# A hybrid gMLP and sparse-attention layer on one core: where cache pages are gathered and output weights are split

## The chip, the core and the metric

The kernel runs on one core of a Trainium2 chip. The metric is the device time of one launch in microseconds (us), the median of three runs. The core has five engines with a queue each: PE (TensorE, matrix products; PEld is its weight load), DVE (VectorE), ACT (ScalarE), POOL (GpSimd) and SP (SyncE), which here issues the DMA transfers. Each engine works through its own queue in order; semaphores tie the queues together. The program's order on each queue is fixed when the program is built.

## The reference, cut to what matters

One inference step of a single layer: 1024 prompt tokens and 8 sample tokens (one new token each, over 256 cached tokens in 2 pages of 128).

```python
hn = rms_norm(x, norm_g)
u, v, z_a, q, kc, vc, ks, vs, kw, vw, gates, z_b = split(hn @ w_in)   # one projection
# group A (gMLP): layer norm of v, spatial gate in chunks of 128 tokens
vn = layer_norm(v, ln_v_g, ln_v_b)
a_out = u * (tril(w_s) @ vn + b_s) * silu(z_a)
# group B (sparse attention): rotated q, ks, kw; compressed k and v; top blocks; window
kcc, vcc = rope(compress(kc, w_ck, pe_ck)), compress(vc, w_cv, pe_cv)
o_b = g0 * attn(q, kcc, vcc) + g1 * attn(q, selected blocks) + g2 * attn(q, window)
mix = concat(a_out, o_b * silu(z_b))
y = rms_norm(x + mix @ w_out, final_g)
# the sample tokens do the same with their cached pages in front:
#   pages(c) = c[page_table]   -> 8 tokens x 2 pages = 16 pages of the four paged caches
```

Outputs are y for prompt and sample, the new k and v rows of each branch, and the normalised v rows of the sample.

## The kernel before, in words

Every fp32 product is done as a split: a tensor is cast to a high part on ACT, the rest is taken by a subtraction (low part), and PE does three matmuls, high by high, low by high and high by low. The work runs in stages:

- up to about 42 us: x is loaded, transposed and split; the first three feature tiles (u and z of group A) are projected. Feature tiles are 128 output columns over all 1032 tokens, in chunks of 344 tokens (`pf`).
- 42 to 117.7 us, the **q stage**: four feature tiles of q. Their weights come in by `load_w` (L133), two loads of 256 KB a tile (`wst<-in_wF`), into a ring of three raw buffers and nine split ones. Each tile is rotated by `rotate` (L297), for which Cq and Sq (cosines and sines, L288) are loaded, and stored to a scratch in DRAM (`qd`, L314). The v weights (`wst<-in_wTv`, eight loads) are fetched in the same stage.
- 117.7 to 216 us, the **v stage**: nine token tiles `ptv` (eight of 128 tokens, one of samples), each of which gets its layer norm (L425 to L431; POOL multiplies by `lng` and adds `lnb`), is split into vh and vl, and goes through `gate` (L393): matmuls `pg` by the lower triangle of w_s, the bias on DVE (L407), the product with u on POOL, and a store of three quarters of it to a scratch `sd` (L412). The constants lng, lnb and w_s are loaded at L349 to L388, behind the stores of the rotated q.
- 190 to 230 us, the **A stage**: token tiles `pta` with ks and kw, rotated in place; each tile's rows go out at L498 and, for the last four, L500. 230 to 270 us, the **B stage**: token tiles `ptb` with the values, gates and raw compressed branch; its weights are `wst<-in_wTb`, eight loads of 204 KB.
- 270 to 324.6 us, **compress** for k and for v (L620), with feature tiles as filler between its steps (`step`, L614); the cached pages (tile `cA`, from the scratch `cg`) are split by POOL at L642. To 366 us the sample's attention.
- 366 to 480 us, attention of query blocks 0 to 3, with feature tiles as filler. 480 to 510 us, the **exchange**: the features are done, their pools close, and the output weights are loaded and split by `load_wo` (L811) into `woh` and `wol`, which take the place of xh and xl. To the end, query blocks 4 to 7 with output projection units (`pout`) as filler.

The cached pages are picked by a page table. SP reads its 16 entries into registers (L294) and issues, for each page, two gathers of 128 KB from DRAM to DRAM, `cg<-in_cA` (L324) and `kg<-in_cB` (L325), four pairs in each q tile, with the instruction `tc.issue_after(W["dma"].ins)`, that is, behind the last weight load issued. A scheduler places other instructions by its own costs, so the queues' order is seen in the built program only.

Of the kernel before, what the change touches and what calls it, by code (L numbers as in the profile page):

```python
# [12 lines left out]
P = 128  # L13
D = 1024
# [25 lines left out]
def trunk(tc, io, outs):  # L40
# [7 lines left out]
    with ExitStack() as top:  # L48
# [26 lines left out]
        cg = dram.tile([2, P, 16, P], F32, name="cg")  # L75
        kg = dram.tile([2, P, 16, P], F32, name="kg")
        qsd = dram.tile([NB, 24], F32, name="qsd")

# [239 lines left out]
        for t in range(4):  # L318
            qF = f_tiles(t)
            wts = f_weights(8 + t) if t else q_first  # L320

            with tc.issue_after(W["dma"].ins):
                for j in range(4 * t, 4 * t + 4):
                    sy.dma_start(cg[:, :, j, :], io["cA"][bass.ds(prow[j], 1)].rearrange("o k p c -> (o k) p c"))  # L324
                    sy.dma_start(kg[:, :, j, :], io["cB"][bass.ds(prow[j], 1)].rearrange("o p (k c) -> (o k) p c", k=2))  # L325
            for k in range(KT):
                f_k(wts, qF, k)
            if t == 1:
                pt = ps_o("pbs")
                for gp in range(4):  # L330
                    pe.transpose(pt[:, gp * P:(gp + 1) * P], bsx.rearrange("p a b -> p (a b)")[:, gp * P:(gp + 1) * P],
                                 ident)
                v.tensor_copy(bsb, pt.rearrange("p (a b) -> p a b", a=4))
            raw = qp.tile([P, TT], F32, tag="raw", bufs=2, name="raw")
            for a, b in zip(views(raw), qF):
                last = s.copy(a, b)  # L336
            if t:
                rotate(t - 1, raws[-1], last)
            raws.append(raw)
        rotate(3, raws[-1], None)  # L340
        qp_ctx.close()
        wq_ctx.close()


# [48 lines left out]
        def gate(i, vh, vl):  # L393
# [17 lines left out]
            g.tensor_tensor(uz[:, 0, cols], uz[:, 0, cols], sp[:, 0, :], op=ALU.mult)  # L411
            sy.dma_start(sd[1:4, :, cols].rearrange("g p c -> p g c"), sp[:, 1:4, :])  # L412

        vn_s = vp.tile([NB, 512], F32, name="vn_s")
        for i in range(9):
# [16 lines left out]
            if i < 8:  # L432
# [3 lines left out]
                v.tensor_tensor(vl, vt, f32(vh), op=ALU.subtract)  # L436
                gate(i, vh, vl)
            else:
                sy.dma_start(outs[14][0, :, 0, :], vn_s)
# [44 lines left out]
        for i in range(9):  # L484
# [12 lines left out]
            rows = slice(i * P, (i + 1) * P)  # L497
            sy.dma_start(o_ks[rows], ka[:, 0:P])  # L498
            if i >= 4:
# [55 lines left out]
        def feature_tiles(bank):  # L555
# [5 lines left out]
            for n, (what, i, _) in enumerate(todo):  # L561
# [5 lines left out]
                for j in range(3):  # L567
# [13 lines left out]
                    if what == "z":  # L581
                        gt = ftp.tile([P, CH], F32, tag="gt", name="gt")
                        sy.dma_start(gt[:, 0:n_p], sd[i, :, cols])
                    z = ftp.tile([P, CH], F32, tag="z", bufs=2, name="z")
                    th = ftp.tile([P, CH], F32, tag="th", name="th")
# [34 lines left out]
        def compress(kv):  # L620
# [17 lines left out]

            def split(dst, src, e=v):
                hi = dst(Xh)  # L640
                s.copy(hi, src)
                e.tensor_tensor(dst(Xl), src, f32(hi), op=ALU.subtract)  # L642
            split(lambda x: x[:, :, 384:388], pce.rearrange("p a j -> p j a"))
# [9 lines left out]
            for h in range(2):  # L653
                split(lambda x: x[:, :, h * SLOT + 64:h * SLOT + 192].rearrange("p j (a m) -> p a j m", m=8),
                      cA[:, :, h * 64:h * 64 + 64].rearrange("p a (m j) -> p a j m", j=8), g)
            pc = ps_p("pc")
            n = 0
            with step(8 if kv == 0 else 12):
              for half in range(2):
# [135 lines left out]
        sm_ctx.close()  # L795
        left = N_FT - (8 + 12 + 4 + 4 + 4 + 12 + 6 + 4)

# [11 lines left out]
        sy.dma_start(cmpm, io["cmpm"])  # L809

        def load_wo(k):  # L811
            st = wop.tile([P, D], F32, tag="wost", name="wost")
            sy.dma_start(st, io["w_out"][k])
            s.copy(woh[:, k, :], st)
            (g if k % 2 else v).tensor_tensor(wol[:, k, :], st, f32(woh[:, k, :]), op=ALU.subtract)

# [296 lines left out]
        for i, (qb, h, tp) in enumerate(todo):  # L1113
            units = [n_values(q) + 2 for q, _, _ in todo[i:] if (q < EARLY) == (qb < EARLY)]
            if 0 <= i - 4 * EARLY < 3:
                units[0] = 0
            if i == 4 * EARLY + 3:
                held_back = blocks[qb]["last"].ins
# [21 lines left out]
            if qb == EARLY - 1:  # L1140
                for _ in fill:
                    pass
                ft_ctx.close()
                wo_ctx = ExitStack()
                wop = wo_ctx.enter_context(tc.tile_pool(name="wop", bufs=7, side="right", reuse_waits="tile"))
                fg = xp.tile([P, D], F32, tag="row", name="fg")
                sy.dma_start(fg, io["final_g"].partition_broadcast(P))
                woh = xp.tile([P, KT, D], F32R, tag="wh", name="woh")
                wol = xp.tile([P, KT, D], F32R, tag="wl", name="wol")
                for k in range(KT):  # L1150
                    load_wo(k)
                wo_ctx.close()
                mixp = top.enter_context(tc.tile_pool(name="mixp", bufs=2, side="right", reuse_waits="tile"))
# [127 lines left out]
```

## Time and profile before

| | |
|---|---|
| median of three runs | 757.92 us (756.63 to 757.99) |
| the profiled execution: its time, its span | 757.39 us, 755.6 us |
| mean granted clock of PE | 0.959 |
| busy: PE, DVE, ACT, POOL | 689.3, 517.2, 373.9, 297.1 us |
| DMA traffic | 78.70 MB, 104 GB/s over the span |

PE is busy for 91% of the span, so the time is PE's work, plus the stretches in which PE stands still, plus what PE loses where its clock is granted at the lower of its two levels. A view by stretches of time shows which stages have such gaps; the views of waits and of the chain say what ended them. A PEclk of 1.00 in such a row is the full clock of 2.4 GHz, 0.50 would be 1.2 GHz all through.

### The profile page before, as it was taken

The numbers are of one execution on the slowest core, as the hardware profiler recorded it, in microseconds if no ns is written. First come the engines' busy times: TensorE is split into PE (matmuls) and PEld (weight loads), VectorE is DVE, ScalarE is ACT, GpSimd is POOL, SyncE is SP. The second block draws the span as 40 slices with busy tenths as digits, with TensorE's granted clock in tenths as the row PEclk, the third lists the DMA queues.
The fourth block names the chain that finished last, engine by engine and source line by source line (L and its number), as shares of the span: only waits on it lengthen the run. The fifth ranks groups of instructions, "written<-read, shape, count | busy, mean of one in ns | idle before, by whom it ended". The sixth has DMA issues, their size and how long they took to land.

```text
span 755.6 us, 12512 instructions
## 1 busy us (share of the span) xinstructions
PE 689.3 (91%) x4186; PEld 635.3 (84%) x4186; DVE 517.2 (68%) x1470; ACT 373.9 (49%) x882; POOL 297.1 (39%) x274
## 2 busy tenths in 40 slices
PE   9996399879999999799899999868999999999994
PEld 7996398768899999698899999757999898988993
DVE  6622296469966155843399989999878786788753
ACT  8410132114225254212377877787666674676631
POOL 0010143154331017442222444478656554375421
PEclk9998689979999999899999999989999999999997
DMA  9153546502234044262533112445123122212011
GB/s 338 52 183 101 157 135 175 146 19 74 69 116 130 26 166 154 61 234 103 147 112 90 62 48 62 160 171 167 44 65 103 43 59 77 52 67 75 19 55 53
DMA packets 61256, 78.70 MB, mean 104 GB/s; under 512 B 5200, under 2 KB 44736, under 8 KB 60392
## 3 DMA queue, kind: packets, MB, share of 16 engines
q1 hardware_dynamic: 60744, 75.48, 31.8%
q0 software_dynamic: 160, 2.15, 0.7%
q8 instruction: 33, 0.54, 0.3%
q14 instruction: 31, 0.25, 0.1%
q10 hardware_dynamic: 288, 0.27, 0.1%
HBM read 59.46 MB, written 24.71 MB: 111 GB/s over the span
## 4 chain that ended last, share of the span: by engine, by line
PE 62%; DVE 13%; SPq 8%; DMA 6%; issue 5%; ACT 3%; POOL 2%; POOLq 0%; DVEq 0%; ACTq 0%
PE pf L45 13%; PE pout L45 11%; PE o L45 8%; PE pt L928 8%; PE S L45 7%; PE ptb L45 5%; SPq L324 4%; PE ptv L45 2%; PE pta L45 2%; DVE tl L932 1%; SPq L139 1%; DVE Pl L847 1%; SPq L325 1%; PE pc L45 1%; PE pg L45 1%
## 5 line engine op out<-in xcount | busy, mean ns | idle before, releaser
L45 PE MATMUL pf<-xh,whi 128*128 128x344 f32 x384 | 111.9, 333 | 11.9 <-ACT raw L336 5.6
L932 DVE TENSOR_TENSOR tl<-pt,th 128x512 fp32r<-128x512 f32 (+1 forms) x160 | 101.2, 643 | 16.6 <-ACT th L931 16.0
L45 PE MATMUL pf<-xl,whi 128*128 128x344 f32 x384 | 111.9, 328 | 0.0
L45 PE MATMUL pf<-xh,wlo 128*128 128x344 f32 x384 | 111.4, 327 | 0.0
L931 ACT CAST th<-pt 128x512 fp32r<-128x512 f32 (+1 forms) x160 | 84.9, 551 | 42.4 <-PE pt L928 37.4
L905 POOL TENSOR_TENSOR Pw<-Pw,r 128x640 f32<-128x640 f32 (+3 forms) x112 | 78.4, 718 | 39.6 <-DVE r L899 23.5
L45 PE MATMUL pout<-woh,mix 128*128 128x512 f32 (+1 forms) x272 | 88.0, 388 | 2.7 <-ACT mix L965 1.8
L45 PEld LDWEIGHTS pf<-xh,whi 128*128 128x128 f32 x384 | 71.4, 194 | 14.3 <-ACT raw L336 5.9
L905 POOL TENSOR_TENSOR Pl<-Pl,r 128x384 f32<-128x384 f32 (+5 forms) x36 | 49.0, 1361 | 80.2 <-DVE r L899 26.2
L45 PE MATMUL o<-th,v 128*128 128x256 f32 x264 | 75.0, 305 | 2.7 <-DVE oT L941 2.7
L142 ACT CAST whi<-wst 128x512 fp32r<-128x512 f32 (+2 forms) x50 | 28.7, 588 | 90.9 <-DMA wst<-in_wF 28.3
L45 PEld LDWEIGHTS pf<-xl,whi 128*128 128x128 f32 x384 | 72.1, 195 | 0.7 <-DVE xl L205 0.3
L45 PE MATMUL o<-tl,v 128*128 128x256 f32 x264 | 70.1, 291 | 2.5 <-DVE tl L932 2.5
L45 PEld LDWEIGHTS pf<-xh,wlo 128*128 128x128 f32 x384 | 71.4, 193 | 0.7 <-issue 0.4
L851 ACT ACTIVATE Pl<-Pl,nmx 128x128 f32<-128x128 f32 (+7 forms) x64 | 49.8, 778 | 23.3 <-DVE nmx L847 18.0
L45 PEld LDWEIGHTS pout<-woh,mix 128*128 128x128 f32 x272 | 50.9, 191 | 11.7 <-ACT mix L965 2.0
L891 ACT ACTIVATE Pw<-Pw,nmx 128x640 f32<-128x640 f32 (+4 forms) x64 | 44.6, 697 | 27.1 <-DVE nmx L883 26.1
L45 PEld LDWEIGHTS o<-tl,v 128*128 128x128 f32 x264 | 51.0, 193 | 5.9 <-DVE tl L932 4.6
L45 PE MATMUL S<-ksS,q 128*128 128x384 f32 (+5 forms) x192 | 53.0, 362 | 3.2 <-DVE nmx L847 1.8
L45 PE MATMUL S<-kwS,q 128*128 128x384 f32 (+2 forms) x224 | 54.0, 337 | 1.6 <-DVE nmx L847 1.5
L45 PEld LDWEIGHTS o<-th,v 128*128 128x128 f32 x264 | 50.9, 193 | 5.0 <-DVE oT L941 3.4
L143 DVE TENSOR_TENSOR wlo<-wst,whi 128x512 fp32r<-128x512 f32 (+2 forms) x32 | 27.7, 886 | 38.7 <-ACT whi L142 38.6
(338 smaller groups left out, 1713.2 us busy)
## 6 DMA issues: line engine op xcount, KB each, us to landing
q<-qd SPq DMA_DIRECT2D x32, 256.0 KB
wst<-in_wF SPq DMA_DIRECT2D x26, 256.0 KB
raw<-in_xw SPq DMA_DIRECT2D x7, 708.0 KB
wost<-in_w_out SPq DMA_DIRECT2D x8, 512.0 KB
xt<-in_x_prompt SPq DMA_DIRECT2D x8, 512.0 KB
out<-xt SPq DMA_DIRECT2D x7, 512.0 KB
cg<-in_cA SPq DMA_DIRECT2D x16, 128.0 KB
kg<-in_cB SPq DMA_DIRECT2D x16, 128.0 KB
```

Of the source, the lines that this page charges most:

```text
L45: return pe.matmul(out, lhsT, rhs, start=start, stop=stop, skip_group_check=True)
L139: W["dma"] = sy.dma_start(st[:, :n], src)
L142: s.copy(hi[:, :n], st[:, :n])
L143: e.tensor_tensor(lo[:, :n], st[:, :n], f32(hi[:, :n]), op=ALU.subtract)
L324: sy.dma_start(cg[:, :, j, :], io["cA"][bass.ds(prow[j], 1)].rearrange("o k p c -> (o k) p c"))
L325: sy.dma_start(kg[:, :, j, :], io["cB"][bass.ds(prow[j], 1)].rearrange("o p (k c) -> (o k) p c", k=2))
L851: s.activation(Pl[:, 0:L], Pl[:, 0:L], AF.Exp, bias=nmx[:, 0:1], scale=-1.0, accum_out=sums[:, 1:2])
L891: s.activation(Pw[:, 0:nw], Pw[:, 0:nw], AF.Exp, bias=nmx[:, 1:2], scale=-1.0, accum_out=sums[:, 2:3])
L905: g.tensor_tensor(t_[:, a:b], t_[:, a:b], r[:, j:j + 1].to_broadcast((P, b - a)), op=ALU.mult)
L928: pe.transpose(pt[:, ci * 256 + e * P:ci * 256 + (e + 1) * P], src[e][:, col:col + P], ident)
L931: s.copy(th[:, :n], pt[:, :n])
L932: v.tensor_tensor(tl[:, :n], pt[:, :n], f32(th[:, :n]), op=ALU.subtract)
```

## The change

1. The 16 pairs of gathers leave the q stage. A new function `gather(j, behind)` issues pair j behind the store of a v tile's gate (pairs 0 to 7) and behind the o_ks store of an A tile (pairs 8 to 15).
2. The output weights are split in the v stage: `split_wo(half, k)`, twice per v tile, loads 256 KB, casts on ACT, subtracts on POOL and stores both parts to a new DRAM scratch `wod` (16 loads and 32 stores of 256 KB). At the exchange `load_wo` is gone, with its pool `wop`; four loads of 2 MB bring both parts back, ahead of the load of final_g.
3. The page splits of compress go from POOL to DVE; the filler of the second compress (v) is 18 feature units in place of 12.
4. The gate's input buffer `gt` has two buffers in place of one, `z` three in place of two. Two attention units in place of three go without filler behind the exchange.

```diff
+        wod = dram.tile([2, 2, P, KT, 512], F32, name="wod")
...
-            with tc.issue_after(W["dma"].ins):
-                for j in range(4 * t, 4 * t + 4):
-                    sy.dma_start(cg[:, :, j, :], io["cA"][bass.ds(prow[j], 1)].rearrange("o k p c -> (o k) p c"))
-                    sy.dma_start(kg[:, :, j, :], io["cB"][bass.ds(prow[j], 1)].rearrange("o p (k c) -> (o k) p c", k=2))
...
+        def gather(j, behind):
+
+            with tc.issue_after(behind.ins):
+                sy.dma_start(cg[:, :, j, :], io["cA"][bass.ds(prow[j], 1)].rearrange("o k p c -> (o k) p c"))
+                sy.dma_start(kg[:, :, j, :], io["cB"][bass.ds(prow[j], 1)].rearrange("o p (k c) -> (o k) p c", k=2))
...
-            sy.dma_start(sd[1:4, :, cols].rearrange("g p c -> p g c"), sp[:, 1:4, :])
+            st = sy.dma_start(sd[1:4, :, cols].rearrange("g p c -> p g c"), sp[:, 1:4, :])
+            gather(i, st)
+
+        def split_wo(half, k):
+
+            cs_ = slice(half * 512, half * 512 + 512)
+            st = vp.tile([P, 512], F32, tag="wost", bufs=2, name="wost")
+            hi = vp.tile([P, 512], F32R, tag="wohi", bufs=2, name="wohi")
+            lo = vp.tile([P, 512], F32R, tag="wolo", bufs=2, name="wolo")
+            sy.dma_start(st, io["w_out"][k, :, cs_])
+            s.copy(hi, st)
+            g.tensor_tensor(lo, st, f32(hi), op=ALU.subtract)
+            sy.dma_start(wod[half, 0, :, k, :], f32(hi))
+            sy.dma_start(wod[half, 1, :, k, :], f32(lo))
...
                 gate(i, vh, vl)
+                for half in range(2):
+                    split_wo(half, i)
...
-            sy.dma_start(o_ks[rows], ka[:, 0:P])
+            st = sy.dma_start(o_ks[rows], ka[:, 0:P])
+            gather(8 + i, st)
...
-                      cA[:, :, h * 64:h * 64 + 64].rearrange("p a (m j) -> p a j m", j=8), g)
+                      cA[:, :, h * 64:h * 64 + 64].rearrange("p a (m j) -> p a j m", j=8))
...
-            with step(8 if kv == 0 else 12):
+            with step(8 if kv == 0 else 18):
...
-        def load_wo(k):
-            st = wop.tile([P, D], F32, tag="wost", name="wost")
-            sy.dma_start(st, io["w_out"][k])
-            s.copy(woh[:, k, :], st)
-            (g if k % 2 else v).tensor_tensor(wol[:, k, :], st, f32(woh[:, k, :]), op=ALU.subtract)
...
-                sy.dma_start(fg, io["final_g"].partition_broadcast(P))
                 woh = xp.tile([P, KT, D], F32R, tag="wh", name="woh")
                 wol = xp.tile([P, KT, D], F32R, tag="wl", name="wol")
-                for k in range(KT):
-                    load_wo(k)
-                wo_ctx.close()
+                for half in range(2):
+                    for hl, w in enumerate((woh, wol)):
+                        sy.dma_start(f32(w[:, :, half * 512:half * 512 + 512]), wod[half, hl])
+                sy.dma_start(fg, io["final_g"].partition_broadcast(P))
```

SP's queue in the q stage. Before, from the last pair of the first q tile on (`wst` is a raw weight buffer, `cg` and `kg` the scratch for pages, an ISA row prepares a register):

```order
L324 DMA cg<-in_cA 256x128
L325 ISA
L325 DMA kg<-in_cB 256x1x128
L139 DMA wst<-in_wF 128x512 x2
L324 ISA
L324 DMA cg<-in_cA 256x128
L325 ISA
L325 DMA kg<-in_cB 256x1x128
```

The same place of SP's queue after the change, from the last read of the page table to the first stores of rotated q:

```order
L140 DMA wst<-in_wF 128x512 x6
L140 DMA wst<-in_wTv 128x512 x5
L280 DMA ud<-uz 128x1032
L140 DMA wst<-in_wTv 128x512 x3
L289 DMA Cq<-in_Cq 128x1032
L290 DMA Sq<-in_Sq 128x1032
L140 DMA wst<-in_wTa 128x384
L315 DMA qd<-qh 64x8x128 x2
```

No gather is left there; the loads of Cq and Sq stand behind six q weight loads and all eight v weight loads, where before the 16 pairs of gathers, six q weight loads and three v weight loads stood ahead of them.

SP's queue at the end of the A stage. Before, from the store of group A's result on (`ka` holds the rotated rows of a tile):

```order
L440 DMA ad<-uz 128x1024
L412 DMA sd<-sp 128x3x128
L139 DMA wst<-in_wF 128x512 x2
L498 DMA out<-ka 128x128
L500 DMA out<-ka 128x128
L139 DMA wst<-in_wF 128x512 x2
L498 DMA out<-ka 128x128
L500 DMA out<-ka 128x128
L498 DMA out<-ka 128x128
L500 DMA out<-ka 128x128
L139 DMA wst<-in_wTb 128x408
```

After the change, a later piece of the same stretch, around three of the B weight loads:

```order
L515 DMA out<-ka 128x128
L343 ISA
L343 DMA cg<-in_cA 256x128
L344 ISA
L344 DMA kg<-in_cB 256x1x128
L518 DMA out<-ka 128x128
L140 DMA wst<-in_wTb 128x408 x3
L140 DMA wst<-in_wF 128x512
L515 DMA out<-ka 128x128
L343 ISA
L343 DMA cg<-in_cA 256x128
```

Between the last gate's `sd` store and the eighth load of `wst<-in_wTb` stand nine pairs of gathers; before, none.

POOL's queue at the start of the v stage, before the change (`wsl` is the low part of the spatial weights, `vt` a v tile):

```order
L430 TENSOR_TENSOR vt<-vt,lng 128x512 x2
L392 TENSOR_TENSOR wsl<-ws,wsh 128x1024
L431 TENSOR_TENSOR vt<-vt,lnb 128x512 x2
```

And after it (`wolo` is the low part of the output weights):

```order
L445 TENSOR_TENSOR vt<-vt,lng 128x512
L425 TENSOR_TENSOR wolo<-wost,wohi 128x512
L445 TENSOR_TENSOR vt<-vt,lng 128x512
L425 TENSOR_TENSOR wolo<-wost,wohi 128x512
L394 TENSOR_TENSOR wsl<-ws,wsh 128x1024
L446 TENSOR_TENSOR vt<-vt,lnb 128x512 x2
```

Two subtractions of output weights stand ahead of `wsl` and of the additions that end the first tile's norm.

## Rows read from the trace of the kernel before

**Rows 1.** Stretches: us, busy PE, PEld, DVE, ACT, POOL, PEclk, DMA, GB/s.

```profile
68.10:75.00 6.90, 6.65 (x27) 6.37 (x27) 0.00 (x0) 0.00 (x0) 0.00 (x0) 0.66 0.25 77
...
84.30:90.50 6.20, 6.14 (x23) 5.90 (x23) 0.00 (x0) 0.00 (x0) 0.00 (x0) 0.55 0.30 104
...
149.00:156.70 7.70, 0.13 (x2) 0.01 (x1) 0.03 (x1) 1.66 (x2) 7.70 (x6) 0.65 0.00 0
...
156.70:216.00 59.30, 56.93 (x311) 51.19 (x312) 55.84 (x154) 16.03 (x32) 24.83 (x23) 0.96 0.20 56
...
240.00:270.00 30.00, 30.00 (x163) 29.71 (x162) 5.91 (x19) 8.85 (x27) 0.00 (x0) 1.00 0.12 33
...
316.00:324.60 8.60, 8.60 (x34) 8.60 (x35) 2.15 (x3) 0.49 (x1) 3.67 (x4) 0.65 0.25 66
...
480.00:535.00 55.00, 43.75 (x265) 36.93 (x264) 53.87 (x157) 42.68 (x100) 39.51 (x34) 0.91 0.52 170
```

**Rows 2.** Waits of PE, 40 to 325 us: total, times, longest.

```profile
PE pbs L331 <- DVE bsx L295: 9.6, 1, 9.6
...
PE pg L45 <- ACT vh L435: 7.9, 2, 7.6
...
PE pf L45 <- ACT raw L336: 5.6, 1, 5.6
...
PE pc L45 <- DVE Xl L642: 5.5, 1, 5.5
...
PE pf L45 <- DVE uz L277: 5.2, 1, 5.2
```

**Rows 3.** Timeline of SP's queue: start, us, instruction.

```profile
50.52 2.31 SPq L324 DMA_DIRECT2D cg<-in_cA  x1
...
53.88 2.31 SPq L324 DMA_DIRECT2D cg<-in_cA  x1
...
56.38 0.67 SPq L325 DMA_DIRECT2D kg<-in_cB  x1
...
91.68 0.38 SPq L288 DMA_DIRECT2D Cq<-in_Cq  x1
...
139.01 1.02 SPq L349 DMA_DIRECT2D lng<-in_ln_v_g  x1
...
216.09 0.82 SPq L412 DMA_DIRECT2D sd<-sp  x1
...
233.04 0.51 SPq L139 DMA_DIRECT2D wst<-in_wTb  x1
```

**Rows 4.** DMA view from 44 to 56 us, 40 slices.

```profile
DMA  9000590154530241021118611111111187111111
...
GB/s 666 0 0 0 219 1533 0 55 185 150 120 75 3 77 121 58 15 63 43 44 56 265 181 55 43 44 43 43 43 44 43 44 242 222 48 44 43 44 43 43
```

**Rows 5.** Timeline of DVE around the rotation of q.

```profile
108.88 1.22 DVE L301 TENSOR_TENSOR raw<-raw,Cq 128x1032 f32<-128x1032 f32 x1
...
129.56 3.45 DVE L301 TENSOR_TENSOR raw<-raw,Cq 128x1032 f32<-128x1032 f32 x1
```

**Rows 6.** POOL's norm products by line: min/median/max ns, first to last.

```profile
L430 POOL TENSOR_TENSOR vt<-vt,lng x8: 1258/1292/1470, 150.0 to 201.9; 128x512 f32<-128x512 f32 x8
```

**Rows 7.** Timeline of DVE in the compress stage.

```profile
302.12 5.63 DVE L675 TENSOR_TENSOR low<-low,Sc 64x384 f32<-64x384 f32 x1
```

**Rows 8.** The tile woh: its splits at the exchange.

```profile
L814 ACT CAST woh<-wost x8: 1047/1066/1077, 489.3 to 502.6; 128x1024 fp32r<-128x1024 f32 x8
...
L815 DVE TENSOR_TENSOR wol<-wost,woh x4: 1607/2178/3416, 491.5 to 504.8; 128x1024 fp32r<-128x1024 f32 x4
...
L815 POOL TENSOR_TENSOR wol<-wost,woh x4: 2355/2378/2387, 493.2 to 508.2; 128x1024 fp32r<-128x1024 f32 x4
```

**Rows 9.** The chain of waits, 205 to 275 us.

```profile
239.99 29.97 PE ptb L45 x161
```

**Rows 10.** DMA view from 490 to 495 us.

```profile
DMA packets 574, 2.09 MB, mean 418 GB/s; under 512 B 64, under 2 KB 64, under 8 KB 574
```

More of the change, by code (lines that the diff above doesn't have):

```diff
@@ L581, in feature_tiles @@
                     if what == "z":
-                        gt = ftp.tile([P, CH], F32, tag="gt", name="gt")
+                        gt = ftp.tile([P, CH], F32, tag="gt", bufs=2, name="gt")
                         sy.dma_start(gt[:, 0:n_p], sd[i, :, cols])
-                    z = ftp.tile([P, CH], F32, tag="z", bufs=2, name="z")
+                    z = ftp.tile([P, CH], F32, tag="z", bufs=3, name="z")
                     th = ftp.tile([P, CH], F32, tag="th", name="th")
@@ L637, in compress, with split @@
             Xl = cx2.tile([P, 8, NSLOT], F32R, tag="Xl", name="Xl")
-            def split(dst, src, e=v):
+            def split(dst, src):
                 hi = dst(Xh)
                 s.copy(hi, src)
-                e.tensor_tensor(dst(Xl), src, f32(hi), op=ALU.subtract)
+                v.tensor_tensor(dst(Xl), src, f32(hi), op=ALU.subtract)
             split(lambda x: x[:, :, 384:388], pce.rearrange("p a j -> p j a"))
@@ L795, in trunk @@
         sm_ctx.close()
-        left = N_FT - (8 + 12 + 4 + 4 + 4 + 12 + 6 + 4)
+        left = N_FT - (8 + 18 + 4 + 4 + 4 + 12 + 6 + 4)
         mk = top.enter_context(tc.tile_pool(name="mk", bufs=1, reuse_waits="tile"))
@@ L1114, in trunk @@
             units = [n_values(q) + 2 for q, _, _ in todo[i:] if (q < EARLY) == (qb < EARLY)]
-            if 0 <= i - 4 * EARLY < 3:
+            if 0 <= i - 4 * EARLY < 2:
                 units[0] = 0
-            if i == 4 * EARLY + 3:
+            if i == 4 * EARLY + 2:
                 held_back = blocks[qb]["last"].ins
@@ L1143, in trunk @@
                 ft_ctx.close()
-                wo_ctx = ExitStack()
-                wop = wo_ctx.enter_context(tc.tile_pool(name="wop", bufs=7, side="right", reuse_waits="tile"))
                 fg = xp.tile([P, D], F32, tag="row", name="fg")
-                sy.dma_start(fg, io["final_g"].partition_broadcast(P))
                 woh = xp.tile([P, KT, D], F32R, tag="wh", name="woh")
                 wol = xp.tile([P, KT, D], F32R, tag="wl", name="wol")
-                for k in range(KT):
-                    load_wo(k)
-                wo_ctx.close()
+                for half in range(2):
+                    for hl, w in enumerate((woh, wol)):
+                        sy.dma_start(f32(w[:, :, half * 512:half * 512 + 512]), wod[half, hl])
+                sy.dma_start(fg, io["final_g"].partition_broadcast(P))
                 mixp = top.enter_context(tc.tile_pool(name="mixp", bufs=2, side="right", reuse_waits="tile"))
```

## The prediction

> **What bounds the kernel now.** I read the table of stretches first [rows 1], since the share of a busy engine over the whole span hides where it stands still. PE is busy through most rows; the gaps lie in four places: the q stage (two rows from 68.1 to 90.5 us, at a granted clock of 0.66 and 0.55), the start of the v stage (149 to 156.7 us, PE busy for 0.13 of 7.7 us), the end of compress (clock 0.65) and the exchange with the first blocks behind it (43.75 of 55 us). The waits of PE say what ended the gaps [rows 2]: in the q stage three single waits of 5.2, 9.6 and 5.6 us, all behind a weight that came late; at the first gate 7.6 us for vh; in compress 5.5 us for Xl. SP's timeline shows why the weights were late [rows 3]: a cg gather holds SP for 2.31 us, its kg for 0.67, and the next pair starts 3.36 us after the last (the cg rows at 50.52 and 53.88). Sixteen pairs cost 16 × 3.36 = 54 us of SP's queue, all ahead of the weights of the next q tile and of Cq.
>
> **Part 1, the q stage.** The queue after the change holds weights alone. The three waits, 20.4 us, have then no cause. PE also loses to its clock: 6.65 us at 0.66 and 6.14 us at 0.55 would be done in 4.4 and 3.4 us at full clock, which is 5.0 us [rows 1]. That is 25.4 us on PE up to the first v tile. The chain of waits runs another way, through SP: Cq, issued at 91.68, feeds the rotation, behind whose last stores lng is issued at 139.01, and the first gate matmul follows at 156.7, the end of the 149 row [rows 1, 3]. After the change Cq stands behind six q and eight v weight loads; the last of these needs a raw buffer, and through it the split weights of the second q tile. PE had that tile nearly done at 62.6 us, before the first of its waits, so I put Cq at about 65 us, 26.7 us earlier. Both ways give 25 to 27; I take −27. Bounds: −16, if Cq waits until the third tile frees its buffers (a tile is 72 matmuls, some 12 us by the 4.4 us for the first row's 27), and −30, if the 7.6 us at the first gate shrinks as well. Against it: on POOL two subtractions now stand ahead of wsl in the order. The nearest rows are POOL's products of the same shape, 1292 ns [rows 6]: 2 × 1.29 = +2.6 us, since POOL was busy through all of 149 to 156.7 [rows 1] and PE waits for it there.
>
> **Part 2, the v stage.** It gets 48 DMAs of 256 KB (2 × 8 loads, 4 × 8 stores), 16 casts on ACT, 16 subtractions on POOL, and eight gather pairs. ACT is 16 of 59 us busy there, so the casts are free. The DMAs: at the 418 GB/s of the best stretch [rows 10] 0.26 MB takes 0.63 us, and 48 take 30 us in a stage of 59 with a DMA share of 0.20. They fit, unless the gathers stand in their way: eight pairs hold SP for 27 us. The POOL subtractions can hurt, for DVE is busy for 55.84 of 59.3 us [rows 1] and is the engine that PE follows there. A DVE product of 128x1032 takes 1.22 us alone and 3.45 beside POOL [rows 5], and a DVE product in compress took 5.63 us while POOL was in a split [rows 7]. So each of 16 subtractions may hold DVE up by anything from nothing to its own 1.29 us: 0 to 20.6 us. POOL already has 24.8 us of work there and DVE still gets 94% busy, so part of the existing lock is in that number, and of the new one DVE's single-input instructions and PSUM reads hide much. I take +5, from 0 to +12, and keep +20 as the far end.
>
> The Trainium skill speaks to this place: "SBUF — State Buffer", section "Who interferes with whom", says that a DVE instruction with two SBUF inputs contends with a GpSimd instruction that reads SBUF, and that whoever issues first holds the shared port for its whole instruction. The trace agrees [rows 5, 7]. By that rule in full the term would be the far end, 20.6 us, and the sum 759.6 (rival E).
>
> **Part 3, the A stage.** Here the change adds a wait. Behind the last `sd` store (216.09 before; call it T) SP had little to do, and it issued the last weight load of the B stage at 233.04, T + 17 [rows 3]; at 239.99 the weight was split and PE ran on for 29.97 us without a gap [rows 9], to T + 54. In the order after the change nine pairs stand between the two: 9 × 3.36 = 30.2 us. Beside them SP has some 14 row stores, four B and four feature weight loads at about 0.4 to 0.5 us each, 11 us, and waits that were inside the 17: T + 41 to T + 47, I take 44. With the same 7 us for landing and splitting, PE gets the last weight at T + 51. It does not stand still all that time: in the order three of nine `pta` tiles and 77 of the 208 `ptb` matmuls stand ahead of the first that needs this weight. The other 131 take 131 × 29.97 / 161 = 24.4 us: T + 75.4, against T + 54. That is +22 us (rounded up from 21.5). PE's own work up to there is about 22 us, so some 25 us of waiting lie bare and the clock may fall in them. Bounds: +10, if row stores waited on PE before and the gathers now fill these waits; +28, if the clock falls and late pages hold up compress.
>
> The gathers are slow for a reason that the move doesn't touch. During a pair the DMA share is 0.1 and the rate 43 to 44 GB/s [rows 4]; 131 KB at 43.5 GB/s is 3.0 us, which is the pace of the pairs. The skill's "DMA: Bandwidth & Descriptors", section "Why a DMA increments its semaphore by 16 and not by 1", says that a transfer is spread over the largest number of engines, up to 16, that divides the slowest dimension of both of its sides; a gather's is 2, so two engines, and the trace agrees with 0.1 of 16. This speaks against the change: by it a pair costs SP the same 3.4 us wherever it stands.
>
> **Part 4, compress.** Without POOL's splits the DVE product of 5.63 us falls back to under 1.2 us (a larger one alone took 1.22 [rows 5]), and PE's wait of 5.5 us for Xl goes [rows 2, 7]; after it PE worked 8.60 us at a clock of 0.65, 3.0 us lost [rows 1]. Together −8.5 at most; the four page splits on DVE, at the 1.22 us of a product of that size [rows 5], give 4.9 back, of which I leave 1.5 on the path: −7, from −8.5 to 0. The six extra feature units move work forward and are nothing by themselves; they fill what gap is left.
>
> **Part 5, the exchange.** PE is idle for 11.3 us of the 55 and loses about 5 to the clock (0.91) [rows 1]. DVE is busy for 53.87 of 55: it is the bound. The splits there cost DVE 4 × 2.18 = 8.7, POOL 4 × 2.38 = 9.5 and ACT 8 × 1.07 = 8.5 us [rows 8], and all go: −9 by DVE's share. In place of 4.2 MB SP fetches 8.4 MB; at 418 GB/s [rows 10] 20 us in place of 10, hidden because the first output projection comes only when attention has taken up the place behind. Bounds: −16 (the whole gap), and +5 if the q load queued behind the 8.4 MB is late by half of the extra 10 us.
>
> **The sum.** −27 + 2.6 + 5 + 22 − 7 − 9 = −13.4 us on the profiled execution's 757.39 us, whose span is 755.6; 744.0. The median of the runs, 757.92, is 0.5 above it, less than the runs' own spread.
>
> **The rivals.**
> - B, slower: the gathers, with two engines at work for 3.0 us a pair, are as dear in their new places as in the old. In the A stage the weight comes at the far end, +28. In the v stage they take 8 × 3.0 = 24 us of these two engines, beside 30 us for their share of the 48 transfers, 54 of 59 us; the output weight loads land late, ACT, which works in order, waits for them ahead of the next tile's eviction, and the term is +17 (24 less the 7.7 us in which PE waits anyway). −27 + 2.6 + 17 + 28 − 7 − 9 = +4.6, 762. It decides where the A and v stages together cost over 40 us. For it: nine pairs ahead of one weight, and 43 GB/s whatever else is in flight. Against: in the v stage a transfer has a whole tile of time, 7.4 us.
> - E, slower as well: POOL's lock on DVE costs the v stage the full 20.6 us, as worked out above: 759.6. Against it: DVE is there at 94% with POOL's 24.8 us of work already beside it.
> - C, the gathers are hidden in the A stage: stores before spent their time in waits for the rotation, PE has 22 us of its own work, and a shorter queue leaves +4 for A, +3 for v: −27 + 2.6 + 3 + 4 − 7 − 9 = −33.4, 724. Against it: the order with nine pairs ahead of a load.
> - D, the exchange gives nothing: PE waits there for DVE's softmax chain either way, or the 8.4 MB come late. −13.4 + 9 = −4.4, 753.
>
> **How the numbers follow.** Forecast 52%, own range 735 to 753; B 14%, E 6%, C 18%, D 10%. The time is 744; the range 724 to 763 takes in C, B and E. A measurement can tell no change within 0.2%, 1.5 us. Faster: 0.49 of the forecast, 0.18 of C, 0.09 of D and 0.01 of E, 0.77; same 0.05, from D, E and the forecast's upper end; slower 0.18, nearly all of B and E.
>
> **What would show it.** In the profile after: the q stage with no wait over 2 us and Cq issued near 65 us, first v matmul near 92; if Cq stands near 80, part 1 is wrong. In the A stage a wait of PE for a `wTb` weight of 20 us or more with SP's gathers ahead of it in the queue; if the waits there are under 8 us, C holds. Two-input DVE rows of 1.5 us and more throughout the v stage would speak for E, ACT waiting for wost for B. At the exchange, PE busy for over 50 of 55 us, or else D. The whole is wrong if the time lies above 757 us with the q stage's waits gone.

## The result and the profile after

The changed kernel takes 751.43 us (median of 18 runs, 748.48 to 757.51) against 758.33 before (18 runs), a ratio of 0.991 with a 95% interval of 0.989 to 0.994. The forecast was 744.0: the sign is right, the gain is about half of what was forecast. The profiled execution has a span of 749.7 us against 755.6, so 5.9 us are to be placed.

The table of stretches after the change (columns as in [rows 1]) is cut at the events of the kernel: first v matmul, first gate, last gate, last B matmul, end of the sample's attention, first output projection, end; the row from 123 us on is the last piece before the first gate.

```profile
38.00:93.90 55.90, 53.44 (x340) 53.09 (x339) 36.99 (x47) 16.23 (x30) 13.92 (x9) 0.97 0.50 156
...
123.00:135.00 12.00, 4.63 (x21) 3.42 (x19) 0.06 (x1) 4.02 (x7) 12.00 (x9) 0.82 0.47 153
...
135.00:203.90 68.90, 59.25 (x293) 52.31 (x294) 53.93 (x132) 20.26 (x38) 40.33 (x35) 0.88 0.65 209
203.90:280.30 76.40, 58.92 (x306) 55.17 (x305) 25.94 (x83) 22.01 (x61) 5.72 (x5) 0.91 0.36 110
...
372.30:520.10 147.80, 140.28 (x1004) 133.58 (x1002) 130.65 (x527) 111.57 (x345) 64.11 (x88) 1.00 0.48 153
```

The same two stretches of the kernel before, v stage and A and B stage, and its attention up to the first output projection:

```profile
156.70:214.90 58.20, 55.83 (x304) 50.09 (x305) 54.79 (x152) 16.03 (x32) 24.37 (x22) 0.96 0.19 54
214.90:267.00 52.10, 52.10 (x304) 51.56 (x304) 20.60 (x63) 20.48 (x55) 5.87 (x5) 1.00 0.32 98
...
363.60:534.90 171.30, 157.20 (x1085) 147.72 (x1083) 153.96 (x563) 127.09 (x371) 83.70 (x100) 0.97 0.36 112
```

The q stage is full now: 53.44 of 55.90 us busy at a clock of 0.97, where before two rows stood at 0.66 and 0.55 with gaps around them. The v stage went from 58.2 to 68.9 us for about as many matmuls, with 9.7 us of idle PE and a clock of 0.88. The A and B stage went from 52.1, without any idle time, to 76.4 us, 17.5 of them idle. Events, in us, for this kernel and those run below (a duration runs from the start of one event to that of the next; `ptb` is the last prompt matmul of the B stage):

| kernel | median | first gate | to last gate | to last ptb | to end of sample attention | to the end |
|---|---|---|---|---|---|---|
| before | 758.33 | 156.7 | 58.1 | 51.9 | 96.9 | 392.0 |
| after | 751.43 | 135.0 | 68.8 | 76.2 | 92.3 | 377.4 |
| e1 gathers reshaped | 730.77 | 134.2 | 65.5 | 59.5 | 92.1 | 376.4 |
| e2 gathers in q stage | 753.57 | 161.3 | 64.3 | 56.8 | 92.4 | 378.1 |
| e3 old output split | 748.19 | 129.5 | 58.4 | 74.9 | 92.7 | 391.0 |
| e4 old page splits, 12 units | 761.67 | 134.0 | 70.0 | 76.7 | 94.5 | 385.9 |
| e5 e1 + old output split | 729.06 | 131.7 | 55.9 | 58.1 | 92.5 | 391.4 |
| e6 e1 + subtractions on DVE | 729.63 | 130.7 | 65.7 | 61.4 | 92.1 | 377.5 |
| e7 e1 + four buffers | 723.74 | 133.3 | 59.5 | 59.9 | 91.9 | 377.8 |
| e8 before + gathers reshaped | 734.04 | 132.6 | 58.9 | 51.8 | 95.0 | 391.2 |
| e9 e7 + gathers in q stage | 729.42 | 137.5 | 61.8 | 57.8 | 92.1 | 380.6 |
| e10 after + four buffers | 744.82 | 133.2 | 62.5 | 76.7 | 92.7 | 378.8 |
| e11 12 units | 754.70 | 134.2 | 69.9 | 75.9 | 89.8 | 384.3 |
| e12 page splits on POOL | 757.07 | 131.9 | 69.7 | 78.2 | 96.9 | 378.0 |

(The last five columns are of one profiled execution each and sum to its span; medians are of 5 to 18 runs. The ten kernels that share the q stage of the changed one issue Cq at anything from 67.7 to 70.7 us, so a difference of under 3 us in the column of the first gate need not come from the edit. The kernel before had a median of 757.0 to 757.2 us beside e1 to e12, and 758.33 beside the changed kernel; a difference between the changed kernel and one of these is good to about 1 us.)

The waits of PE from 38 to 330 us after the change:

```profile
PE pg L45 <- ACT vh L450: 9.9, 2, 7.4
PE ptb L45 <- ACT whi L143: 8.5, 4, 3.1
PE pkt L524 <- DVE k L521: 8.4, 2, 7.0
...
PE pc L45 <- DVE Xl L660: 2.6, 2, 1.7
```

The three waits of the q stage in [rows 2] are gone. The one at the first gate, 7.4 us, stands as it did (7.6). New ones are those for B weights and for rotated keys (`k`). SP's timeline after the change:

```profile
70.46 0.42 SPq L289 DMA_DIRECT2D Cq<-in_Cq  x1
...
113.40 1.13 SPq L351 DMA_DIRECT2D lng<-in_ln_v_g  x1
...
207.77 0.39 SPq L414 DMA_DIRECT2D sd<-sp  x1
...
222.38 0.67 SPq L344 DMA_DIRECT2D kg<-in_cB  x1
223.16 2.19 SPq L515 DMA_DIRECT2D out<-ka  x1
225.55 0.56 SPq L343 DMA_DIRECT2D cg<-in_cA  x1
...
253.41 1.94 SPq L140 DMA_DIRECT2D wst<-in_wTb  x1
```

Cq and lng come 21.2 and 25.6 us earlier than in [rows 3]. From the last `sd` store to the last B weight load SP now takes 45.6 us, where it took 17. A gather itself holds SP for 0.6 us here; it is the next DMA, whatever it is, that is held, the row store for 2.19 us. From one cg to the next, where one row store or two stand between, it is 3.3 to 4 us, the old price. The chain of waits through this stretch (start, us, what):

```profile
210.26 6.39 DMA ctok<-in_ctok
...
227.10 5.15 DMA out<-ka
...
240.65 5.06 DMA out<-ka
...
253.41 4.67 DMA wst<-in_wTb
...
258.69 23.69 PE ptb L45 x126
```

A row store of 64 KB takes up to 5 us to land behind the gathers, ACT waits for its buffer (12.6 us in four waits), and in the end PE waits for the last B weight; the 126 matmuls behind it were forecast as 131 with 24.4 us and took 23.69.

The first piece of this chain is a load that neither the change's description nor the forecast mentions: `ctok`, the cosines by which the A tiles are rotated. Before the change it went out among the constants of the v stage; now it stands behind the last output weight store and a pair of gathers (the first line is of the kernel before, the second of this one):

```profile
143.00 0.35 SPq L466 DMA_DIRECT2D ctok<-in_ctok  x1
...
210.26 3.12 SPq L483 DMA_DIRECT2D ctok<-in_ctok  x1
```

DVE's first rotation waits 9.7 us for it, and the wait of 7.0 us for `k` is PE's behind it. The load is late in every kernel below that splits the output weights in the v stage (198.7 us or later), and early in those that split them at the exchange (e3 116.0, e5 118.3, e8 119.5).

In the v stage the tile of raw output weights, `wost`, shows what its engines waited for (us, times):

```profile
  DMA wost<-in_w_out: 48.4, 12
  ACT wohi L424: 18.0, 6
```

Of the 48.4 us, 30.8 in nine waits lie behind the first gate, the rest ahead of it. ACT's timeline in the v stage (in brackets the idle time before, and what ended it):

```profile
153.11 0.62 ACT L424 CAST wohi<-wost 128x512 fp32r<-128x512 f32 x1 [11.18 <-DMA wost<-in_w_out]
...
163.49 0.62 ACT L424 CAST wohi<-wost 128x512 fp32r<-128x512 f32 x1 [5.05 <-DMA wost<-in_w_out]
...
171.30 0.63 ACT L450 CAST vh<-vt 128x512 fp32r<-128x512 f32 x1 [4.82 <-POOL vt L446]
```

ACT is busy for 20 of 69 us, and yet it stands for 11 us in front of one cast, with the casts `vh` that the next gates need and the evictions of the next v tiles (`vt`) queued behind.

Ahead of the first gate the output weights stand in the queues of POOL and ACT as well (`vt<-vt,lnb` is the addition that ends a tile's norm):

```profile
125.99 1.29 POOL L425 TENSOR_TENSOR wolo<-wost,wohi 128x512 fp32r<-128x512 f32 x1
...
128.47 1.26 POOL L425 TENSOR_TENSOR wolo<-wost,wohi 128x512 fp32r<-128x512 f32 x1
...
131.99 2.47 POOL L446 TENSOR_TENSOR vt<-vt,lnb 128x512 f32<-128x512 f32 x2
...
133.77 0.62 ACT L424 CAST wohi<-wost 128x512 fp32r<-128x512 f32 x1 [2.41 <-DMA wost<-in_w_out]
134.29 1.14 ACT L450 CAST vh<-vt 128x512 fp32r<-128x512 f32 x2
```

The first half of the tile was ready at 133.24, halfway through the additions, and its cast `vh` came 1.1 us later, behind `wohi`. From the issue of lng to the first gate it is 21.6 us, where before it was 17.7.

At the exchange the row of the 55 us up to 5 us behind the first output projection stands beside that of 480 to 535 us before [rows 1]:

```profile
470.00:525.00 55.00, 49.43 (x340) 43.88 (x340) 50.05 (x190) 42.88 (x117) 34.93 (x40) 1.00 0.82 269
```

PE is idle for 5.6 us of it in place of 11.3, at the full clock.

### The profile page after: what moved, and what is told of

It is laid out like the page before. It is cut to its first block, busy times and chain, and to the rows that moved or that the text cites. A ratio compares the mean times of both kernels' runs of the same rounds, so it can differ in the third digit from the quotient of the medians.

```text
span 749.7 us, 12604 instructions
## 1 busy us (share of the span) xinstructions
PE 688.4 (92%) x4186; PEld 631.7 (84%) x4186; DVE 514.1 (69%) x1470; ACT 374.6 (50%) x890; POOL 293.8 (39%) x282
## 4 chain that ended last, share of the span: by engine, by line
PE 53%; DVE 14%; DMA 13%; issue 6%; SPq 5%; ACT 4%; POOL 4%; POOLq 0%; ACTq 0%; DVEq 0%
PE pf L45 15%; PE pout L45 10%; PE o L45 7%; PE S L45 6%; PE pt L940 6%; PE ptb L45 3%; DMA wost<-in_w_out 3%; DMA out<-ka 2%; PE pc L45 2%; DMA wst<-in_wF 1%; DMA wst<-in_w_c 1%; DVE Xl L660 1%; DVE Pl L859 1%; PE po L45 1%; DMA qd<-sh 1%
## 5 line engine op out<-in xcount | busy, mean ns | idle before, releaser
L45 PE MATMUL pf<-xh,whi 128*128 128x344 f32 x384 | 109.4, 326 | 2.1 <-ACT xh L205 1.2
L45 PE MATMUL pf<-xl,whi 128*128 128x344 f32 x384 | 109.9, 322 | 0.0
L45 PE MATMUL pf<-xh,wlo 128*128 128x344 f32 x384 | 109.8, 323 | 0.0
L917 POOL TENSOR_TENSOR Pw<-Pw,r 128x640 f32<-128x640 f32 (+3 forms) x112 | 76.1, 699 | 52.5 <-DVE r L911 28.0
L917 POOL TENSOR_TENSOR Pl<-Pl,r 128x384 f32<-128x384 f32 (+5 forms) x36 | 49.3, 1369 | 76.7 <-DVE r L911 30.0
L45 PEld LDWEIGHTS pf<-xh,whi 128*128 128x128 f32 x384 | 69.7, 189 | 3.7 <-ACT xh L205 2.1
L45 PEld LDWEIGHTS pf<-xl,whi 128*128 128x128 f32 x384 | 70.3, 190 | 1.0 <-issue 0.6
L45 PEld LDWEIGHTS pf<-xh,wlo 128*128 128x128 f32 x384 | 69.9, 189 | 0.3 <-issue 0.2
L45 PE MATMUL o<-tl,v 128*128 128x256 f32 x264 | 69.7, 289 | 0.4 <-DVE tl L944 0.3
L45 PE MATMUL S<-ksS,q 128*128 128x384 f32 (+5 forms) x192 | 51.8, 357 | 2.4 <-DMA q<-qd 1.9
L45 PE MATMUL pout<-wol,mix 128*128 128x512 f32 (+1 forms) x136 | 52.5, 387 | 0.0
L144 POOL TENSOR_TENSOR wlo<-wst,whi 128x512 fp32r<-128x512 f32 x18 | 24.1, 1342 | 70.0 <-ACT whi L143 51.5
```

What stands on the lines that cost most here:

```text
L45: return pe.matmul(out, lhsT, rhs, start=start, stop=stop, skip_group_check=True)
L144: e.tensor_tensor(lo[:, :n], st[:, :n], f32(hi[:, :n]), op=ALU.subtract)
L917: g.tensor_tensor(t_[:, a:b], t_[:, a:b], r[:, j:j + 1].to_broadcast((P, b - a)), op=ALU.mult)
```

## The experiments

### e1: the gathers reshaped

The lines are shortened here; `cA[page]` and `cB[page]` stand for the indexed inputs.

```diff
-  cg[:, :, j, :], cA[page].rearrange("o k p c -> (o k) p c")
+  cg[:, :, j, :].rearrange("k p c -> p k c"), cA[page].rearrange("o k p c -> (o p) k c")
-  kg[:, :, j, :], cB[page].rearrange("o p (k c) -> (o k) p c", k=2)
+  kg[:, :, j, :].rearrange("k p c -> p k c"), cB[page].rearrange("o p (k c) -> (o p) k c", k=2)
```

> The changed kernel with one edit: both gathers of a pair are written with the 128 page rows as the slowest dimension in place of the 2 halves; same bytes, same order on every queue. Theory 1 (the added time of the v and A stages is the price of gathers that hold SP for 3.4 us a pair and move their 128 KB at 43 GB/s): the pair's hold on SP falls under 1.5 us, last gate to last ptb matmul falls from 76 us to under 60 us (52 before the change), first to last gate matmul from 69 us toward 63, and the time to 725 to 735 us. Theory 2 (the v stage is held by ACT waiting for the 16 output weight loads because 48 transfers of 256 KB fill the DMA engines, gathers or not): A falls as said but the v stage stays within 2 us of 69, time 733 to 738. Theory 3 (the A stage waits for its row stores and buffers, not for SP): A stays within 5 us of 76 and the time above 747.

730.77 us, ratio to before 0.966 (0.963 to 0.968). The A and B stage falls from 76.2 to 59.5 us, the v stage from 68.8 to 65.5:

```profile
134.20:199.80 65.60, 57.98 (x292) 51.28 (x293) 55.31 (x134) 20.24 (x38) 41.30 (x35) 0.90 0.69 223
199.80:259.50 59.70, 55.62 (x306) 52.36 (x305) 24.76 (x81) 22.30 (x61) 5.76 (x5) 0.97 0.46 137
```

Theory 1 holds for the A stage and for the time; theory 3 falls. In the v stage 3.3 us go and most of the added time stays, nearer to theory 2.

### e2: the gathers back in the q stage

The q stage's loop issues its four pairs a tile again, as the removed lines of the diff do; the two calls of `gather` go.

> The changed kernel with the 16 pairs of gathers put back into the q stage; output weight split, DVE page splits and the rest stay. By the working of the prediction the q stage loses its 24 us again, and the A stage gives back its 24. Theory 1: the v stage also gives back the gathers' part (first to last gate 69 to about 63 us), time 744 to 748. Theory 2 (output weight traffic alone): v stays at 67 to 69 us and the time at 750 to 753. Theory 3: the A stage (76 us from last gate to last ptb matmul) stays over 70, and the time rises to 765 to 775.

753.57 us, 0.994 (0.992 to 0.997). The first gate is late again (161.3), the A and B stage gives back 19.4 of 24.3 us, and the v stage, without a gather in it, still takes 64.3 us. Theories 1 and 2 are both part of it: of the 10.7 us about 4.5 go with the gathers, 6.2 stay with the output weights. What the move of the gathers alone is worth is the difference to the changed kernel, 2 us, and the intervals of the two ratios overlap (0.992 to 0.997 and 0.989 to 0.994), so it isn't shown to be more than nothing. The 4.9 us by which the A and B stage stays above that of before, with no gather in it, are waits of PE: 3.3 us for rotated keys, 2.3 of them behind the late `ctok` (DVE waits 4.0 us for it), the rest nearly all for split weights. No run moved `ctok` by itself.

### e3: the output weights split at the exchange again

```diff
-                for half in range(2):
-                    split_wo(half, i)
...
+                for k in range(KT):
+                    load_wo(k)
```

> The changed kernel with the output weights loaded and split at the exchange as before, gathers where the change has them. The exchange loses the 9.5 us that the profiles give it (idle and clock between 478 and 535 us before, 470 and 520 after). Theory 2 (the v stage's added 11 us are the 48 transfers and 32 casts and subtractions): first to last gate falls from 69 to 58 to 60 us and the first gate comes 2 us earlier, so the time is 747 to 751, no worse than the changed kernel. Theory 1 (the gathers): the v stage falls by under 5 us and the time is 755 to 759.

748.19 us, 0.988 (0.985 to 0.990), 3 us less than with the change, with intervals that overlap: in this kernel the move of the output split was worth nothing, if not less. Theory 2 holds, even a little beyond its forecast: with the gathers still in it the v stage is back at 58.4 us (before: 58.1), and the first gate comes 5.5 us earlier, of which 4.1 lie behind the issue of lng (17.5 us from there to the gate, against 21.6). The rest, from the end of the sample's attention on, grows by 13.6 us.

```profile
129.50:188.00 58.50, 53.40 (x285) 48.46 (x286) 51.34 (x149) 15.92 (x32) 23.30 (x22) 0.92 0.27 80
188.00:263.00 75.00, 58.89 (x324) 56.45 (x324) 21.01 (x66) 20.57 (x55) 5.58 (x5) 0.91 0.35 103
```

The stage holds 285 matmuls here against 304 before, so it isn't quite the old one. With the gathers reshaped as well (e5) it takes 55.9 us with 286: slow gathers cost the v stage about 2.5 us without the output weights, and 4.5 beside them (e2).

### e4, e11, e12: the page splits and the filler

```diff
-                      cA[...].rearrange("p a (m j) -> p a j m", j=8))
+                      cA[...].rearrange("p a (m j) -> p a j m", j=8), g)
...
-            with step(8 if kv == 0 else 18):
+            with step(8 if kv == 0 else 12):
```

e4 has both edits, e12 the first alone, e11 the second alone (with the count `left` of the units that remain).

> The changed kernel with the page splits of compress on POOL again and 12 feature units of filler in its second half. If the compress term of the prediction holds (-7, of which the profiles show 7 to 8), the time is 757 to 760 us and PE waits 4 us or more for Xl. The rival (the extra filler units only move work, and the lock on DVE lies beside other waits of this later stage): 750 to 753 us.

> The changed kernel with 12 filler units in the second half of compress as before; page splits stay on DVE. e4 undid both and cost 10 us. If the units are what fills PE there (and what lets the features end before the exchange), the time is 756 to 760; if POOL's splits were the cost, 751 to 753.

> The changed kernel with the page splits back on POOL and the 18 filler units kept: the other half of e4. If POOL's lock on DVE is the compress term, 757 to 760 us; if the filler covers it, 751 to 754.

e4: 761.67 us, 1.005 (1.003 to 1.007), slower than before; the rival falls, and the price is above the forecast 757 to 760. e12: 757.07, 1.000 (0.997 to 1.002), 5.6 us above the changed kernel, as the first of its two forecasts has it; e11: 754.70, 0.997 (0.995 to 0.999), 3.3 above, between its two forecasts. Together 8.9, and e4 is 10.2 above; by the ratios to the kernel before it is 6.2 and 4.5 against 10.4, so the two prices add up, and the six units are worth something by themselves. With POOL's splits the stage to the end of the sample's attention takes 96.9 us in place of 92.3, and PE waits for Xl for 3.7 and 0.9 us (2.6 in all in the changed kernel). The timelines of POOL and DVE in e12 show the lock on two products that take at most 1.0 and 0.54 us in the changed kernel:

```profile
296.35 3.06 POOL L660 TENSOR_TENSOR Xl<-cA,Xh 128x1024 fp32r<-128x1024 f32 x1
296.83 4.38 DVE L644 TENSOR_TENSOR w<-wst,w 128x512 fp32r<-128x512 f32 x1
...
310.38 6.59 POOL L660 TENSOR_TENSOR Xl<-cA,Xh 128x1024 fp32r<-128x1024 f32 x2 [0.42 <-ACT Xh L659]
...
315.43 1.97 DVE L693 TENSOR_TENSOR low<-low,Sc 64x384 f32<-64x384 f32 x1
```

On DVE, in the changed kernel, such a split takes some 2.2 us:

```profile
296.24 2.17 DVE L660 TENSOR_TENSOR Xl<-cA,Xh 128x1024 fp32r<-128x1024 f32 x1
```

With 12 units (e11) that stage is 2.5 us shorter, but the six units left over come back behind it: to the end it takes 6.9 us more.

### e5: e1 with the old output split

> Gathers on the page-row dimension as in e1, and the output weights loaded and split at the exchange as before. In e3 (old split, slow gathers) the v stage fell by 10 us and the first gate came 4 us earlier, and the time from the sample's attention to the first output projection grew by 13. Theory 2a (ACT, which works in order, waits for output weight loads ahead of the v tiles' own casts; this costs the v stage some 7 us and the first gate 4 with fast gathers too): last gate near 184 us after 200 in e1, then 13 us given back at the exchange: 726 to 731 us. Theory 2b (with fast gathers the loads land in time and the split costs the v stage nothing more): 735 to 744 us.

729.06 us, 0.962 (0.960 to 0.965). Last gate at 187.6 us after 199.7 in e1, the rest 15 us longer: theory 2a, and the two ways to place the split are worth the same within the runs' spread as long as it has two buffers.

### e6: the subtractions on DVE

```diff
-            g.tensor_tensor(lo, st, f32(hi), op=ALU.subtract)
+            v.tensor_tensor(lo, st, f32(hi), op=ALU.subtract)
```

> As e1, but the 16 subtractions that give the low part of the output weights run on DVE and not on POOL. Rival E of the prediction (POOL's lock holds DVE up in the v stage): DVE takes 16 x 0.7 us = 11 us more work, but without the lock first to last gate falls from 65.5 to under 62 us, 725 to 729 us. Theory 2a (ACT's queue waits for loads; the lock is a small part): the stage stays at 64 to 68 us, as DVE is busy nearly all through it, and the time at 729 to 736.

729.63 us, 0.965 (0.962 to 0.968), within the spread of e1. First to last gate 65.7 us against 65.5: no gain, though DVE took 11 us of work in exchange, so this run alone doesn't price the lock. The first gate comes 3.5 us earlier (130.7), but lng 1.9 us earlier too, on a part of the program that the edit leaves alone; 1.6 us are left for POOL's subtractions ahead of `wsl`.

### e10, e7: four buffers for the raw output weights

```diff
-            st = vp.tile([P, 512], F32, tag="wost", bufs=2, name="wost")
+            st = vp.tile([P, 512], F32, tag="wost", bufs=4, name="wost")
```

e10 is the changed kernel with this edit alone, e7 is e1 with it.

> The changed kernel, gathers as they are, with four buffers for the raw output weights. Theory 2a alone: ACT's 48 us of waits for these loads fall under half, first to last gate from 69 to about 62 us, the time to 744 to 746. Rival, theory 1 (with slow gathers in the same queue the loads are late however many buffers there are): 749 to 752, first to last gate over 66.

> As e1, with four buffers in place of two for the raw output weights, so that a load can be issued two tiles' halves ahead. Theory 2a: ACT's waits for these loads (41.6 us in e1) fall under 25 us, first to last gate falls from 65.5 to 60 to 63 us, and the time to 724 to 728. Rival (the transfers themselves are late, 48 of 256 KB beside the stores, however early they are issued; or the first gate's chain, which has four casts ahead of it, decides): no change, 729 to 732.

e10: 744.82 us, 0.983 (0.980 to 0.986), 6.6 below the changed kernel. e7: 723.74, 0.956 (0.954 to 0.959), the fastest of all. Theory 2a holds, and with slow gathers too. e7's v stage is nearly as short as that of before:

```profile
133.30:192.90 59.60, 56.17 (x297) 49.27 (x298) 53.76 (x132) 20.52 (x38) 43.03 (x36) 0.95 0.71 233
```

The tile `wost` in e10:

```profile
L423 SPq DMA_DIRECT2D wost<-in_w_out x16: 327/423/493, 117.0 to 168.8; - x16
...
  DMA wost<-in_w_out: 16.2, 4
```

The last load is issued at 168.8 in place of 195.2 us, ACT waits for 16.2 in place of 48.4 us (behind the first gate 5.6 in place of 30.8), and the two stretches of e10 show where that arrives:

```profile
133.20:195.80 62.60, 55.87 (x298) 50.06 (x298) 51.87 (x132) 20.92 (x38) 42.04 (x36) 0.94 0.68 222
195.80:272.70 76.90, 58.91 (x301) 55.81 (x300) 25.37 (x83) 22.06 (x61) 5.61 (x5) 0.87 0.35 106
```

The v stage is 6.3 us shorter, the A and B stage as long as ever, with its gathers.

### e8: the kernel before, gathers reshaped

The edit of e1, in the kernel before and its q stage.

> The kernel before, with its gathers in the q stage written with the page rows as the slowest dimension. If the q stage's 24 us are the hold of slow gathers on SP (16 x 3.4 us), Cq is issued near 70 us in place of 91.7, first v matmul near 94, and the time is 732 to 738 us without any move. If the stage is held by the number of transfers or by the weights' own landing, the time stays above 748.

734.04 us, 0.970 (0.968 to 0.973). A pair now holds SP for 1.5 us, and Cq goes out at 68.92:

```profile
53.08 0.59 SPq L324 DMA_DIRECT2D cg<-in_cA  x1
53.85 0.54 SPq L325 DMA_DIRECT2D kg<-in_cB  x1
54.58 0.57 SPq L324 DMA_DIRECT2D cg<-in_cA  x1
...
68.92 0.39 SPq L288 DMA_DIRECT2D Cq<-in_Cq  x1
```

Over four pairs the mean rate is 232 GB/s, at a DMA share of 0.83, where it was 43 to 44 GB/s at a share of 0.1 [rows 4] (the view of 53 to 59.4 us):

```profile
DMA packets 2247, 1.49 MB, mean 232 GB/s; under 512 B 142, under 2 KB 1990, under 8 KB 2246
q1 hardware_dynamic: 2246, 1.47, 82.6%
```

So the q stage's gaps were the price of the gathers' shape. One edit to two access patterns, with nothing moved, is worth 23 us, more than three times the change.

### e9: the best parts together

e7 with the reshaped gathers left in the q stage.

> What the runs point to: gathers on the page rows and left in the q stage as before the change, four buffers for the raw output weights, the rest as changed (split in the v stage, page splits on DVE, 18 filler units). Theory 1 with 2a: in e7 the time from the last gate to the last B matmul is still 60 us against 52 before the change, with gathers and row stores mixed in SP's queue; with the gathers gone from there it is 52 to 55, the q stage stays as short as in e8, and the time is 716 to 721 us. Rival (the 8 us there come from matmuls that were moved in behind the last gate or from the output weight stores, not from gathers): 722 to 726.

729.42 us, 0.963 (0.960 to 0.966): the rival, and worse than that. The A and B stage takes 57.8 us without a gather in it; what keeps it 6 us above the 51.9 of before is in part the late `ctok` (DVE waits 3.9 us for it, PE 2.3 behind that), and otherwise was not separated (its matmuls are 298 against 304; PE waits for 4.5 us there in all, where before it had no wait). And the first gate is 4.2 us later than in e7. With a pair at 1.5 us the q stage isn't the better place.

## Why the forecast was half right

- **Part 1, the q stage: right.** −27 was forecast for the chain through Cq and lng; e3, in which no output weight stands ahead of the first gate, has that gate at 129.5, 27.2 us earlier. Cq was put at 65 and came at 70.5, and lng still moved by 25.6.
- **Its POOL term: right, but not all there is.** +2.6 was forecast for two subtractions ahead of `wsl`, and in POOL's timeline they take 1.29 and 1.26 us there. From lng to the first gate the change costs 3.9 us (17.7 to 21.6); of the rest about 1.1 is ACT, whose cast at 133.77 stands ahead of the first `vh` cast. ACT has four such casts there, and I didn't count them.
- **Part 2, the v stage: the term that was mis-sized.** "ACT is 16 of 59 us busy there, so the casts are free" and "They fit, unless the gathers stand in their way" gave +5; it measured +10.7, and with the first gate the split costs 15.9 us up to the last gate (203.8 against 187.9 in e3; 14.5 counted from lng on) where I had 7.6. The step that failed is the one that took an engine's idle share for free time. For an engine that works in order the busy share wasn't the price: twelve of the 16 `wohi` casts waited for a transfer, and with two buffers the transfer can be issued only when POOL has done with the one before the last. Rival B named this wait, and its sign, ACT waiting for `wost`, came true, but B had it as a price of the gathers; e2 has it without them (36.1 us), e3 has the gathers without it. With four buffers (e10) the kernel takes 744.8 us, near the 744.0 that was forecast with these loads in time, and the v stage is 4.4 us above before, against +5; that the whole agrees so closely is in part luck, as its A stage is 2.8 us dearer than forecast and its last two parts 1.4 cheaper.
- **POOL's lock, rival E: wrong for the v stage.** In e7 all 16 subtractions are on POOL and first to last gate is 59.5 us, 1.4 above before (with 297 matmuls against 304). The rule of the Trainium skill that spoke for it, "SBUF — State Buffer", section "Who interferes with whom", holds where the trace shows the lock (4.38 us in e12, [rows 7]). By it in full the v stage would have cost 20.6 us; the 1.4 us bear no such price out.
- **Part 3, the A stage: right in size, and in the main in mechanism.** +22 was forecast, from the last `sd` store on; from there the last prompt matmul moved from T + 50.6 (266.7) to T + 72.2 (280.0, T at 207.77), 21.6 us. From the last gate it is 24.3, since that store came later behind its gate. Nine pairs put the last weight at T + 45.6 (T + 44 forecast). Reshaping the gathers takes 16.7 of the 24.3 us away (e1), taking them out 19.4 (e2); the forecast gave the gathers all of it. Of the 4.9 us left, 2.3 are a wait behind the late `ctok`, a price of the output split that no term has; the rest stays open. The sign that I had named, a wait of 20 us or more for a `wTb` weight, didn't come: the 17.5 idle us of PE are eight waits of at most 7.0 us, 8.5 us in all for B weights and 8.4 for rotated keys, as the row stores and `ctok` stood behind gathers too. The rule of the Trainium skill cited for it, "DMA: Bandwidth & Descriptors", section "Why a DMA increments its semaphore by 16 and not by 1", gives both the fault and the cure: with 128 as the slowest dimension on both sides 16 engines may take part. The runs agree: the pair's hold falls from 3.4 to 1.5 us and the rate rises to 232 GB/s (e8). I used it against the change and didn't draw its other half, that the shape was there to be changed. Rival C falls. Rival B wanted over 40 us from the A and v stages together; they cost 35.0, where the forecast had 27.
- **Parts 4 and 5: right in kind, each mis-sized, close together by luck.** −16 was forecast. Compress and sample attention gained 4.6 us (96.9 to 92.3) with six more units done in them, the rest 14.6 (392.0 to 377.4) with six fewer: −19.2. Part 4's −7 was too much: the page splits are worth 5.6 us by e12, PE still waits for Xl for 2.6 us, and a split on DVE takes 2.2 us, not the 1.22 that I had from a product of about that size. Its statement that the six units "are nothing by themselves" was wrong: e11 prices them at 3.3 us. Part 5's −9 was too little: e3 gives the exchange 13.6, within its bound of −16 (whose "about 5" for the clock is 3.9 by 43.75 us at 0.91). PE is busy for 49.4 of 55 us there, just under the 50 that I had named as the sign, and DVE for 50.1. No wait for `woh` or `wol` shows, so the 8.4 MB didn't come late; rival D falls.

By the events: −21.7 + 10.7 + 24.3 − 4.6 − 14.6 = −5.9 us of span. The forecast's terms for these are −24.4, +5, +22 and −16 together. The missing 7.5 us are the 8.4 by which the last gate comes later than forecast (2.7 at the first gate, 5.7 in the v stage, for the most part the output split) and the A stage (2.3), against 3.2 more from the last two.

## What to carry to other kernels

When a transfer is slow, look first at what makes it slow and only then at where it stands: moving 16 slow gathers was worth some 2 us, which the runs don't tell from nothing, and reshaping them in place 23. When work is put into a stage for its idle engines, count the waits it brings into their in-order queues besides its busy time, and give a load that such a queue waits for enough buffers to be issued ahead.

## What was not expected of the hardware

The hold of a gather on SP shows at whatever DMA stands next in the queue: 1.1 to 3.1 us at row stores, weight loads or output weight stores after the change, while the cg row itself fell from 2.31 to 0.56 us. A line's own duration on SP is thus not its price. The same bytes in the same 512-byte rows, with 128 in place of 2 as the slowest dimension, brought the pair from 3.4 to 1.5 us of SP's time. Row stores of 64 KB issued behind gathers took up to 5.2 us to land, and ACT, which wanted their buffers, waited for 12.6 us in four waits.
